# Expert weights of a mixture-of-experts layer loaded as 16 KB rows per partition, contraction reordered to match

## The chip, the cores and the metric

One core of one Trainium2 chip runs the whole kernel. The metric is the device time of one execution in microseconds (us); the kernel before has 1452.36 us as the median of three runs (1451.78 to 1454.26). Engines are named as the profile names them: PE is TensorE's products, PEld its loads of the stationary operand, DVE VectorE, ACT ScalarE, POOL GpSimd, SP the engine whose queue issues the loads from HBM.

## What is computed

One sequence of 256 tokens with 1,024 features, all in float32, passes an attention layer with two branches, a mixture of 32 experts, a gated embedding, and then a second block of two layers. The change touches the experts:

```python
def routed_experts(h, w_router, b_router, w_gate_up, b_gate_up, w_down, b_down):
    logits = hf @ w_router + b_router
    top_vals, top_idx = lax.top_k(logits, 4)          # 4 of 32 experts per token
    top_w = jax.nn.softmax(top_vals, axis=-1)
    ...                                               # rows of 64 tokens per expert
    gu = xb @ w_gate_up[e] + b_gate_up[e]             # [64,1024] @ [1024,2048]
    g, u = gu[:, :1024], gu[:, 1024:]
    g, u = jnp.minimum(g, 7.0), jnp.clip(u, -7.0, 7.0)
    glu = g * jax.nn.sigmoid(1.702 * g)
    yr = ((u + 1.0) * glu) @ w_down[e] + b_down[e]    # [64,1024] @ [1024,1024]
    ...                                               # weighted sum back to the tokens
```

## The kernel before

The 256 tokens are two tiles (`NT`) of 128 rows; X is their residual stream, XS the normed rows (token on the partition, feature along the row). The stage of the experts goes over all 32 in turn, each with one block of 64 rows (`SL`); experts with more rows get further blocks in a loop behind the stage, whose count is known only on the chip.

For an expert e, `expert` first asks for its weights with `load`. `load` (L167) cuts a matrix of 128-row blocks into tiles and issues a DMA for each on SP's queue: for gate and up one block of 128 rows x 2,048 columns makes a tile of 1 MB, 8 KB in each partition; for down two blocks of 128 x 1,024 make one, two runs of 4 KB in each partition. So an expert has 8 + 4 tiles. In the stage they come from a ring of 17 tiles (`raw_slot`, pool `ring2`), opened where the pool `p1` of the first phase is closed: a ring tile lies over that pool's buffers and waits until these are left. A pool of the next phase, `p3`, then lies over the ring. The first weights of the gated embedding (`w_ple_gate`, loaded at L193 in `load_split`) are scaled by ScalarE into its buffers (L198).

`gather` (L773) makes, for each token tile, a 0/1 matrix OH of token by row, and multiplies XS by it: for each of the 8 groups k of 128 features, `XS[:, t, k*P:(k+1)*P]` is the stationary operand [128 x 128] and OH the moving one [128 x 64]. The 16 products of an expert (32 records of PE in the trace, two for each) leave the features of group k on the partitions. DVE multiplies them by the gain `g_ffn` (L782) into XG. The gather of expert e+1 is issued behind the gate/up products of expert e; on PE it stands between the transposes of u and the products with down.

The gate/up products take XG[:, k] (64 columns) as stationary operand and halves of 512 columns of the weights as moving one, 8 x 4 = 32 products, in bank pG for gate and pU for up, behind a product with the biases (BIAS). The lower 64 partitions of a bank hold columns 0 to 511, the upper ones 512 to 1,023. VectorE and ScalarE make u from them; PE transposes the routing weights OW (L810) and four pieces of u (L823, `u[:, c*P:(c+1)*P]`), and 16 products with down follow. `combine` (L835) multiplies the result by the transposed weights and VectorE adds it to X (L840).

All operands are float32. In the trace the names right of the arrow are the moving and the stationary operand: `bank<-raw,mid` is a product with weights, `bulk<-OH,XS` the gather, `bank<-cst,mid` the transposes of u, `bulk<-mid,small` combine. The order on the engines is a scheduler's: it takes instructions of the program in order, but those under `issue_after` behind a marked one. Behind experts 18 and 22 come two extra pieces (`down_biases`, `further_list`); in the last but one expert the products of `w_ple_proj`.

Of the kernel before, what the change touches and what calls it, by code (L numbers as in the profile page):

```python
# [22 lines left out]
SL = 64  # L23
# [6 lines left out]
# columns of the constants that depend on shapes alone  # L30
# [4 lines left out]
# columns of the small vectors (feature k * 128 + p at partition p, column k)  # L35
COLS = (("g_mix", 8), ("c_2", 8), ("mla_q_lat_norm", 2), ("mla_kv_lat_norm", 1), ("g_ffn", 8), ("g_ple", 8),
        ("g_pre_2", 16), ("b_ada_2", 48), ("pool_scale_2", 8), ("w_conv_2", 24), ("mla_q_norm", 1), ("mla_k_norm", 1))
# [5 lines left out]
# rows that every partition gets  # L43
# [31 lines left out]
def layouts(inp):  # L75
    """The small inputs and the activations, laid out by partition."""
    def by_part(n):
        v = inp[n].reshape(-1)
        if v.size == QK:  # the rotated part of the heads has its gains in the rope tables
            v = np.concatenate([v[:NOPE], np.ones(P - NOPE, np.float32)])  # L80
        return v.reshape(-1, P).T

    rows = np.concatenate([inp[n].reshape(-1) for n, _ in ROWS])
    post = np.stack([inp["g_post_2"], inp["b_ada_2"][:, 2 * D:]], 1)
    return {
        "cst": constants(),
        "xT": np.ascontiguousarray(inp["x"][0].T.reshape(KD, P, S).transpose(1, 0, 2)),
        "pT": np.ascontiguousarray(inp["p"][0, 0].T.reshape(2, P, S).transpose(1, 0, 2)),
        "cols": np.ascontiguousarray(np.concatenate([by_part(n) for n, _ in COLS], 1)),
        "rows": np.ascontiguousarray(np.broadcast_to(rows, (P, R_N))),  # L90
        "post": np.ascontiguousarray(post),
    }
# [3 lines left out]
def block_kernel(ctx: ExitStack, tc: tile.TileContext, a, out, dbg=None, ne=NE):  # L96
# [19 lines left out]
    def pair(at=None):  # L116
        """Room for the halves of 1024 columns."""
        if at is not None:
            return at if isinstance(at, list) else (at[:, 0:1024], at[:, 1024:2048])
        if early.get("pair"):  # L120
            return early["pair"].pop(0)
        return [phase["pool"].tile([P, 1024], FR, name=n, tag=n, bufs=phase["pairs"]) for n in ("hi", "lo")]

    def raw_slot(n=1024):
        if "ring2" in phase:
            return phase["ring2"].tile([P, 2048], F32, name="raw2", tag="raw2")
        if early.get("raw"):
            return early["raw"].pop(0)
        return phase["pool"].tile([P, 1024], F32, name="raw", tag="raw", bufs=phase["raws"])
# [22 lines left out]
    def mm3(o, l, r, start, stop):  # L152
        """float32 product of operands split in halves of 12 bits each."""
        mm(o, l[0], r[0], start, False)
        mm(o, l[0], r[1], False, False)
        mm(o, l[1], r[0], False, stop)

    def split(raw, dst, eng=None):
        """raw = dst[0] + dst[1], both exact in the tensor engine's short float32."""
        nc.scalar.copy(dst[0], raw)  # L160
        n = raw.shape[-1]
        w = n if eng is None or len(raw.shape) > 2 else min(n, 512)
        for c0 in range(0, n, w):
            cs = slice(c0, min(n, c0 + w))
            (eng or nc.vector).tensor_sub(dst[1][..., cs], raw[..., cs], dst[0][..., cs].bitcast(F32))  # L165

    def load(src, cn, size=2048, at=None):  # L167
        """Rows of src over (k, partition), a tile at a time, in turn in the tiles at where they are given."""
# [14 lines left out]

    def load_split(src, cn, order=None, room=(), eng=None, gains=None, later=None, raws=None):
        """As load, each tile in two halves; with gains, rows by themselves, times those,
        and what makes the low halves in the list later."""
# [24 lines left out]
    tiles = {"adr": [ada_slot() for _ in range(3)]}  # L211
    hh, hl = [slot(s, dt=FR).rearrange("p (k n) -> p k n", k=KD) for s in ("s0", "s1")]
# [4 lines left out]
    wu, vv = slot("s2", 2560), slot("s5")  # L217
# [146 lines left out]
    # the rotated part of the keys that the heads share  # L364
# [6 lines left out]
    def rope(dst, src, T, half_, eng=None):  # L371
        """dst = src * cos + swapped src * sin, for heads [128, heads, 2 * half_] with the table of a token tile."""
# [7 lines left out]
    def head_root(src, hd, extra=None):  # L380
        """(mean of squares + eps) ** -0.5 of the heads [128, heads, d] over hd features."""
        ss, d = tiny([P, H], "ssh"), src.shape[2]
        for h0 in (0, 4):
            sq = mid([P, 4, d])
            nc.scalar.activation(sq, src[:, h0:h0 + 4], AF.Square)
            nc.vector.reduce_sum(ss[:, h0:h0 + 4], sq, axis=AX)
        if extra is not None:
            nc.vector.tensor_scalar(ss, ss, extra, None, op0=OP.add)
        return root(mean_eps(ss, hd, H)).unsqueeze(2)

    roots_a, marks = [], []  # what fills gaps is issued behind the marks
# [32 lines left out]
    # the norm along the tokens, on every partition  # L424
# [61 lines left out]
    def values(hp, prs, Vt, dst):  # L486
        """The values of two heads, feature-major, in halves."""
# [42 lines left out]
    MODC = perm.tile([P, 2, 16], F32, name="MODC")  # L530

    def ada_acc(l, c, e):
        """The products of 512 columns, still to be summed over the partitions."""
# [58 lines left out]
    def branch_weights(n):  # L592
        """A tile for each 256 columns."""
# [5 lines left out]
    # sigmoid(z) = (tanh(z / 2) + 1) / 2; the half follows the output projection  # L599
# [23 lines left out]
    # the biases of gate and up: row p has expert p % 32's, low halves where p // 32 is odd,  # L623
    # the columns h * 512 to h * 512 + 511 of both for h = p // 64
# [31 lines left out]
    def logits(XT, h, pl):  # L656
        """The transposed half of X[:, t] times the router's weights; the norm's factor follows."""
# [72 lines left out]
    def further_list():  # L730
        """The further blocks of 64 rows of the experts that got more than 64."""
# [16 lines left out]
        # a row of the list for each partition that has one: its place, then its expert and first rank  # L748
# [24 lines left out]
    def gather(rank, wgt):  # L773
        OH, OW = [work.tile([P, NT, n], F32, name=s, tag=s, bufs=2) for s, n in (("OH", SL), ("OW", P))]
        pX = bulk()
        for t in range(NT):
            nc.vector.tensor_scalar(OH[:, t], io64, rank(t), None, op0=OP.is_equal)  # L777
            for k in range(KD):
                mm(pX[:, k * SL:(k + 1) * SL], XS[:, t, k * P:(k + 1) * P], OH[:, t], t == 0 and k == 0,
                   t == NT - 1 and k == KD - 1)  # L780
        XG = mid([P, KD, SL])
        nc.vector.tensor_mul(XG, pX.rearrange("p (k n) -> p k n", k=KD), bcol("g_ffn", 0, KD, SL))  # L782
# [6 lines left out]
    def expert(rank, wgt, biassel, gu_src, dn_src, after_gu=None, ready=None, at=None):  # L789
        gu = load(gu_src, 2 * DE, at=at)  # L790
        dn = load(dn_src, D) if at is None else None
# [4 lines left out]
        for k in range(KD):  # L796
            for i, pb in enumerate((pG, pU)):
                for h in range(2):
                    mm(pb[h * SL:(h + 1) * SL], XG[:, k], gu(k, i * DE + h * 512, i * DE + (h + 1) * 512),
# [13 lines left out]
        # what does not wait for the activations of this expert fills their time  # L813
# [6 lines left out]
        dn = dn or load(dn_src, D, at=at)  # L820
        ph = bank()
        for c in range(4):
            nc.tensor.transpose(ph[:, c * P:(c + 1) * P], u[:, c * P:(c + 1) * P], ident)  # L823
# [3 lines left out]
        for j in range(8):  # L827
            for h in range(2):
                mm(py[h * SL:(h + 1) * SL], hT[:, j % 4, (j // 4) * SL:(j // 4 + 1) * SL],
                   dn(j, h * 512, (h + 1) * 512), j == 0, j == 7)  # L830
# [52 lines left out]
    ring2 = tc.tile_pool(name="ring2", bufs=17, reuse_waits="tile")  # L883
    phase.update(ring2=ring2.__enter__())
    for e in range(ne):
        if e == max(ne - 2, 0):
            # of the gated embedding, what does not depend on the experts
            wpp, pT_ = load(a["w_ple_proj"][0], D), raw_slot()[:, :512].rearrange("p (k n) -> p k n", k=2)
# [50 lines left out]
    def split_T(t, dst, src, scale_of=None, bias_of=None):  # L939
        """src(k) of 128 columns each transposed, with per-feature scale and shift, in halves."""  # L940
# [23 lines left out]
    def products(ks, f, turned, late, free=None, behind=None):  # L964
        """The products f(k, h) in an order that frees the weights of the first four k soon,
        the last of them behind the transposes of the tokens before."""
# [32 lines left out]
    def sum_sq(t, ss):  # L999
        """Squares of X[:, t], summed by halves as they come."""  # L1000
# [5 lines left out]
    def normed(l, t, ss, hm):  # L1006
        """The modulated norm of X[:, t], transposed, in halves."""
# [14 lines left out]
    def gates_of(l):  # L1022
        """The weights of the gates that are token-major: the first tokens need not wait for the others."""
# [31 lines left out]
    for l in range(2):  # L1055
# [16 lines left out]
        def gate(dst, g, j):  # L1072
            """dst times feature tile j of the token-major g."""
# [70 lines left out]
        # the gate of the residual, on every partition, times the gains of the last norm  # L1144
# [75 lines left out]
```

## Time and profile before

| | |
|---|---|
| runs, median (lowest to highest) | 1452.36 us (1451.78 to 1454.26) |
| the profiled execution: its own time, the span of its page | 1451.8 us |
| PE busy | 1385.2 us (95%) |
| PEld / DVE / ACT / POOL busy | 795.1 / 594.2 / 319.3 / 320.9 us |
| packets on the main DMA queue | 143,936, with 500.60 MB |
| expert stage, from the first to the last product with expert weights | about 234 to 1185 us |

The page cuts the span into 40 slices of 36.3 us and gives the busy share of each engine in tenths, 9 being 90% or more. Further views list what an engine waited for, its work grouped by form of instruction, its timeline, and the DMA traffic of a stretch. One product of float32 shows as more than one record on PE; a duration "of one" is that of one record and overlaps the next, so the pace is read from starts or from a sum over many.

### The profile page before, as it was taken

Reading aid. Unit: us, or ns where it says so; the run is one execution under the profiler, and the core shown is the slowest. Engines: PE = TensorE matmul, PEld = TensorE weight load, DVE = VectorE, ACT = ScalarE, POOL = GpSimd, SP = SyncE. Lnnn points to the kernel's source line nnn. Section 1 sums busy time; section 2 is a strip of 40 time slices with the busy share of each in tenths; the row PEclk is TensorE's granted clock in tenths of the full one; section 3 lists DMA queues with packets and bytes.
Section 4 is the critical chain, followed back from the end, with each engine's and each line's share of the span. In section 5 each row is a group of like instructions: output and inputs, shape, how many; then the busy total and the mean of one; then the engine's idle time right before and its main releaser. Section 6 shows DMA issues by size and latency. Waiting matters only on the chain. (4 is left out here: it accounts for less than half of the span.)

```text
span 1451.8 us, 18980 instructions
## 1 busy us (share of the span) xinstructions
PE 1385.2 (95%) x7599; PEld 795.1 (55%) x7599; DVE 594.2 (41%) x973; ACT 319.3 (22%) x598; POOL 320.9 (22%) x353
## 2 busy tenths in 40 slices
PE   7989999999999999999999999999999998889987
PEld 6788886344444444444443344444444347887986
DVE  4898954121322132213222222221321138688685
ACT  6745531000000000000000000000001135435432
POOL 5595461000000000000000000000000035785682
PEclk9989998999999999999999999999999999999999
DMA  9738789999999999999999999999999955756651
GB/s 332 239 119 305 263 305 401 417 417 418 417 415 416 418 418 416 415 417 418 418 416 416 417 417 418 417 415 417 417 418 415 417 226 189 232 176 202 202 190 44
DMA packets 144586, 502.56 MB, mean 346 GB/s; under 512 B 10288, under 2 KB 63792, under 8 KB 111472
## 3 DMA queue, kind: packets, MB, share of 16 engines
q1 hardware_dynamic: 143936, 500.60, 88.0%
q8 instruction: 61, 1.00, 0.3%
q10 hardware_dynamic: 560, 0.72, 0.2%
q14 instruction: 29, 0.24, 0.0%
HBM read 500.24 MB, written 1.05 MB: 345 GB/s over the span
## 5 line engine op out<-in xcount | busy, mean ns | idle before, releaser
L150 PE MATMUL bank<-raw,mid 128*64 128x512 f32 x3072 | 680.3, 598 | 1.9 <-ACT mid L825 1.4
L150 PEld LDWEIGHTS bank<-raw,mid 128*64 128x64 f32 x3072 | 215.1, 138 | 414.9 <-issue 387.9
L803 DVE TENSOR_SCALAR mid<-bank 128x512 f32<-128x512 f32 x32 | 22.1, 691 | 443.7 <-PE bank L150 443.7
L855 POOL CAST BIAS<-BIAS 128x128 fp32r<-128x128 f32 x32 | 10.2, 321 | 852.5 <-PE bank L150 852.4
L165 DVE TENSOR_TENSOR lo<-raw,hi 128x1024 fp32r<-128x1024 f32 (+2 forms) x91 | 116.1, 1296 | 21.3 <-ACT hi L160 20.9
L150 PE MATMUL bulk<-OH,XS 128*128 128x64 f32 x1024 | 121.6, 278 | 1.6 <-DVE OH L777 1.6
L150 PEld LDWEIGHTS bulk<-OH,XS 128*128 128x128 f32 x1024 | 120.2, 196 | 2.6 <-DVE OH L777 1.8
L160 ACT CAST hi<-raw 128x1024 fp32r<-128x1024 f32 (+1 forms) x102 | 105.8, 1041 | 68.0 <-PE bulk L150 57.5
L805 ACT ACTIVATE mid<-mid 128x512 f32<-128x512 f32 x32 | 20.1, 629 | 390.6 <-DVE mid L803 390.6
L150 PE MATMUL bulk<-mid,small 64*128 64x512 f32 x256 | 99.2, 628 | 7.1 <-DVE X L840 6.4
L784 DVE TENSOR_SCALAR OW<-cst,RM,SW 128x128 f32<-128x128 f32 x64 | 19.3, 344 | 172.1 <-PE bank L810 172.1
L840 DVE TENSOR_TENSOR X<-X,bulk 128x512 f32<-128x512 f32 x128 | 81.7, 679 | 9.0 <-PE bulk L150 9.0
L165 POOL TENSOR_TENSOR lo<-raw,hi 128x512 fp32r<-128x512 f32 x50 | 72.9, 1484 | 40.1 <-ACT hi L160 35.3
L812 ACT COPY small<-bank 128x256 f32<-128x256 f32 x32 | 11.9, 372 | 290.2 <-PE bank L810 290.2
L150 PEld LDWEIGHTS bulk<-mid,small 64*128 64x128 f32 x256 | 31.0, 185 | 74.8 <-issue 40.4
L150 PE MATMUL bulk<-hi,s 128*128 128x256 f32 (+2 forms) x256 | 59.3, 323 | 7.9 <-ACT hi L160 7.4
L150 PE MATMUL bulk<-s,hi 128*128 128x256 f32 x320 | 63.7, 296 | 0.0
L782 DVE TENSOR_TENSOR mid<-bulk,VC 128x512 f32<-128x512 f32 x32 | 22.1, 691 | 90.9 <-PE bulk L150 90.9
L556 DVE SCALAR_TENSOR_TENSOR acc<-adr,cact,acc 128x512 f32<-128x512 f32 x49 | 55.5, 1133 | 0.8 <-DMA adr<-in_w_ada_dram 0.3
L150 PEld LDWEIGHTS bulk<-s,hi 128*128 128x128 f32 x320 | 51.8, 197 | 1.0 <-DVE s L609 0.4
L559 POOL TENSOR_TENSOR adr<-adr,cact 128x512 f32<-128x512 f32 x32 | 44.5, 1412 | 34.3 <-DMA adr<-in_w_ada_dram 34.3
L150 PEld LDWEIGHTS bulk<-hi,s 128*128 128x128 f32 x256 | 43.9, 195 | 11.6 <-ACT hi L160 7.4
(442 smaller groups left out, 1906.0 us busy)
## 6 DMA issues: line engine op xcount, KB each, us to landing
raw<-in_w_gate_up_dram SPq DMA_DIRECT2D x256, 1024.0 KB, 19.8
raw<-in_w_down_dram SPq DMA_DIRECT2D x128, 1024.0 KB, 20.0
raw<-in_w_in_dram SPq DMA_DIRECT2D x75, 512.0 KB, 5.1
adr<-in_w_ada_dram SPq DMA_DIRECT2D x48, 512.0 KB, 4.5
raw<-in_w_out_dram SPq DMA_DIRECT2D x23, 512.0 KB, 3.8
raw<-in_w_ple_gate_dram SPq DMA_DIRECT2D x5, 512.0 KB, 15.8
raw<-in_w_branch_b_dram SPq DMA_DIRECT2D x4, 512.0 KB, 7.3
raw<-in_w_branch_a_dram SPq DMA_DIRECT2D x4, 512.0 KB, 5.4
```

What stands on the lines that cost most here:

```text
L150: nc.tensor.matmul(o, l, r, start=start, stop=stop)
L160: nc.scalar.copy(dst[0], raw)
L165: (eng or nc.vector).tensor_sub(dst[1][..., cs], raw[..., cs], dst[0][..., cs].bitcast(F32))
L556: e.scalar_tensor_tensor(v, w[:, k], cact[:, i + k:i + k + 1], v, op0=OP.mult, op1=OP.add)
L559: e.tensor_mul(w[:, k:k + 2], w[:, k:k + 2], cact[:, i + k:i + k + 2].unsqueeze(2).to_broadcast([P, 2, n]))
L782: nc.vector.tensor_mul(XG, pX.rearrange("p (k n) -> p k n", k=KD), bcol("g_ffn", 0, KD, SL))
L784: nc.vector.tensor_scalar(OW[:, t], io64d, rank(t), wgt(t), op0=OP.is_equal, op1=OP.mult)
L803: nc.vector.tensor_scalar(g_, pG, 7.0, None, op0=OP.min)
L805: nc.scalar.activation(sg, g_, AF.Sigmoid, scale=1.702)
L812: nc.scalar.copy(OT, pT[:, :S])
L840: nc.vector.tensor_add(xv, xv, pc)
L855: nc.gpsimd.tensor_copy(bs, ONE[:, e, :, None].bitcast(F32).to_broadcast([P, 2, SL]))
```

## The change

The rows of an expert's matrices are dealt to the partitions in another way. `load_rows` gives partition p of block b the r rows that follow each other in HBM, from row (128 b + p) r on: two rows of 2,048 for gate and up, four rows of 1,024 for down, 16 KB in one run in both cases. A tile is 2 MB, an expert has 4 + 2 tiles, and the ring has 8 tiles of 16 KB per partition in place of 17 of 8 KB. The inner dimension of a product is summed over partitions and over j in the tile, so the other operand must follow the same order: `gather` takes every second column of XS (`k // 2 * 256 + k % 2`, step 2), the gain that scales XG is laid out likewise (`g_rows`, 8 new columns in VC), and the transposes before down take every fourth column of u. The further blocks load pieces of 8 KB per partition as before, in the new order. `vv` and `wu` are allocated earlier in `p1`, so their place changes; `w_ple_proj` and pT share one ring tile. Comments are gone, so line numbers move by 2 to 23.

```diff
+        if n == "g_rows":
+            return inp["g_ffn"].reshape(4, P, 2).transpose(1, 0, 2).reshape(P, KD)
...
-            return phase["ring2"].tile([P, 2048], F32, name="raw2", tag="raw2")
+            return phase["ring2"].tile([P, 4096], F32, name="raw2", tag="raw2")
...
+    def load_rows(src, cn, r, at=None):
+        blocks = src.rearrange("(b p r) n -> b p r n", p=P, r=r)
+        nb, parts = src.shape[0] // (P * r), {}
+        pr = r if at is None else 2048 // cn
+        def piece(b, i):
+            if (b, i) not in parts:
+                raw = (raw_slot() if at is None else at[len(parts) % len(at)])[:, :pr * cn]
+                raw = raw.rearrange("p (r n) -> p r n", r=pr)
+                nc.sync.dma_start(raw, blocks[b, :, i * pr:(i + 1) * pr])
+                parts[b, i] = raw
+            return parts[b, i]
+        if at is None:
+            for b in range(nb):
+                piece(b, 0)
+        return lambda b, j, c0, c1: piece(b, j // pr)[:, j % pr, c0:c1]
...
+    vv, wu = slot("s5"), slot("s2", 2560)
...
-    wu, vv = slot("s2", 2560), slot("s5")
...
-                mm(pX[:, k * SL:(k + 1) * SL], XS[:, t, k * P:(k + 1) * P], OH[:, t], t == 0 and k == 0,
+                mm(pX[:, k * SL:(k + 1) * SL], XS[:, t, k // 2 * 256 + k % 2:(k // 2 + 1) * 256:2], OH[:, t], t == 0 and k == 0,
...
-        nc.vector.tensor_mul(XG, pX.rearrange("p (k n) -> p k n", k=KD), bcol("g_ffn", 0, KD, SL))
+        nc.vector.tensor_mul(XG, pX.rearrange("p (k n) -> p k n", k=KD), bcol("g_rows", 0, KD, SL))
...
-        gu = load(gu_src, 2 * DE, at=at)
-        dn = load(dn_src, D) if at is None else None
+        gu = load_rows(gu_src, 2 * DE, 2, at)
+        dn = load_rows(dn_src, D, 4) if at is None else None
...
-                    mm(pb[h * SL:(h + 1) * SL], XG[:, k], gu(k, i * DE + h * 512, i * DE + (h + 1) * 512),
+                    mm(pb[h * SL:(h + 1) * SL], XG[:, k], gu(k // 2, k % 2, i * DE + h * 512, i * DE + (h + 1) * 512),
...
-            nc.tensor.transpose(ph[:, c * P:(c + 1) * P], u[:, c * P:(c + 1) * P], ident)
+            nc.tensor.transpose(ph[:, c * P:(c + 1) * P], u[:, c::4], ident)
...
-                   dn(j, h * 512, (h + 1) * 512), j == 0, j == 7)
+                   dn(j // 4, j % 4, h * 512, (h + 1) * 512), j == 0, j == 7)
...
-    ring2 = tc.tile_pool(name="ring2", bufs=17, reuse_waits="tile")
+    ring2 = tc.tile_pool(name="ring2", bufs=8, reuse_waits="tile")
...
-            wpp, pT_ = load(a["w_ple_proj"][0], D), raw_slot()[:, :512].rearrange("p (k n) -> p k n", k=2)
+            pr = raw_slot()
+            wpp, pT_ = load(a["w_ple_proj"][0], D, at=[pr[:, :2048]]), pr[:, 2048:2560].rearrange("p (k n) -> p k n", k=2)
```

On SP's queue one expert's loads in the middle of the stage, before:

```order
L176 DMA raw_5013<-in_w_gate_up_dram 128x2048
L176 DMA raw_5015<-in_w_gate_up_dram 128x2048
L176 DMA raw_5017<-in_w_gate_up_dram 128x2048
L176 DMA raw_5019<-in_w_gate_up_dram 128x2048
L176 DMA raw_5021<-in_w_gate_up_dram 128x2048
L176 DMA raw_5023<-in_w_gate_up_dram 128x2048
L176 DMA raw_5025<-in_w_gate_up_dram 128x2048
L176 DMA raw_5027<-in_w_gate_up_dram 128x2048
L176 DMA raw_5029<-in_w_down_dram 128x2x1024
L176 DMA raw_5031<-in_w_down_dram 128x2x1024
L176 DMA raw_5033<-in_w_down_dram 128x2x1024
L176 DMA raw_5035<-in_w_down_dram 128x2x1024
```

The same expert in the changed kernel:

```order
L197 DMA raw_5203<-in_w_gate_up_dram 128x4096
L197 DMA raw_5205<-in_w_gate_up_dram 128x4096
L197 DMA raw_5207<-in_w_gate_up_dram 128x4096
L197 DMA raw_5209<-in_w_gate_up_dram 128x4096
L197 DMA raw_5211<-in_w_down_dram 128x4096
L197 DMA raw_5213<-in_w_down_dram 128x4096
```

Twelve issues become six, in the same order, and nothing stands between the experts in either.

On PE, from combine of one expert to the first gate/up product after the next biases (names with a number are ring tiles), before:

```order
L150 MATMUL bulk<-mid,small 128x512 x4
L823 MATMUL bank<-cst,mid 128x128 x4
L150 MATMUL bulk<-OH,XS 128x64 x16
L150 MATMUL bank<-raw_4892,mid 64x512 x4
L150 MATMUL bank<-raw_4894,mid 64x512 x4
L150 MATMUL bank<-raw_4896,mid 64x512 x4
L150 MATMUL bank<-BIAS 128x512 x2
L810 MATMUL bank<-cst,OW 128x128 x2
L150 MATMUL bank<-raw_4898,mid 64x512 x4
L150 MATMUL bank<-raw_5013,mid 64x512 x4
```

The same place in the changed kernel:

```order
L152 MATMUL bulk<-mid,small 128x512 x4
L845 MATMUL bank<-cst,mid 128x128 x4
L152 MATMUL bulk<-OH,XS 128x64 x16
L152 MATMUL bank<-raw_5336,mid 64x512 x8
L152 MATMUL bank<-raw_5338,mid 64x512 x8
L152 MATMUL bank<-BIAS 128x512 x2
L832 MATMUL bank<-cst,OW 128x128 x2
L152 MATMUL bank<-raw_5453,mid 64x512 x8
```

The last quarter of down (raw_4898) stood behind the biases and the transposes of OW; as the second half of the tile raw_5338 it now stands before them.

## Rows read from the trace of the kernel before

**Rows 1.** The page: first line, and busy tenths of two engines
```profile
span 1451.8 us, 18980 instructions
...
PE   7989999999999999999999999999999998889987
...
DMA  9738789999999999999999999999999955756651
```
**Rows 2.** Waits of PE, 240 to 1185 us (total us, times, longest)
```profile
PE bulk L150 <- DVE X L840: 6.4, 31, 0.2
...
PE bank L150 <- DVE small L744: 0.4, 1, 0.4
```
**Rows 3.** PE's work by form, 320 to 1080 us (busy us, ns, idle)
```profile
L150 PE MATMUL bank<-raw,mid 128*64 128x512 f32 x2472 | 546.0, 597 | 0.0
```
**Rows 4.** Waits of SP's queue from 500 to 600 us
```profile
SPq L176 <- DMA raw<-in_w_gate_up_dram: 33.5, 19, 2.1
```
**Rows 5.** Timeline of PE, expert stage (start us, length us, operation, count)
```profile
484.36 3.68 PE L150 MATMUL bulk<-OH,XS 128*128 128x64 f32 x32
...
494.15 15.67 PE L150 MATMUL bank<-raw,mid 128*64 128x512 f32 x72
...
512.99 0.66 PE L823 MATMUL bank<-cst,mid 128*128 128x128 f32 x4
513.49 3.68 PE L150 MATMUL bulk<-OH,XS 128*128 128x64 f32 x32
```
**Rows 6.** DMA packets of two stretches, 779 to 794 and 767 to 774 us
```profile
DMA packets 946, 6.25 MB, mean 417 GB/s; under 512 B 96, under 2 KB 96, under 8 KB 272
...
q1 hardware_dynamic: 945, 6.23, 100.4%
...
DMA packets 658, 2.90 MB, mean 415 GB/s; under 512 B 44, under 2 KB 44, under 8 KB 563
...
q1 hardware_dynamic: 658, 2.90, 102.8%
```
**Rows 7.** Timeline of SP's queue: DMA issues, first expert and about 728 us
```profile
186.74 19.06 SPq L176 DMA_DIRECT2D raw<-in_w_gate_up_dram  x8
...
727.81 17.42 SPq L176 DMA_DIRECT2D raw<-in_w_gate_up_dram  x8
```
**Rows 8.** Timeline of PE, first expert's begin, expert 18's combine
```profile
217.54 1.91 PE L652 MATMUL bank<-cst,X 128*128 128x128 f32 x16
...
234.32 6.04 PE L150 MATMUL bank<-raw,mid 128*64 128x512 f32 x20 [0.57 <-DVE mid L782]
...
771.91 1.98 PE L150 MATMUL bulk<-mid,small 64*128 64x512 f32 x6
```
**Rows 9.** DMA issues, 238-258 and 727-746 us (count, KB, us to landing)
```profile
raw<-in_w_down_dram SPq DMA_DIRECT2D x4, 1024.0 KB, 10.5
...
raw<-in_w_gate_up_dram SPq DMA_DIRECT2D x8, 1024.0 KB, 20.8
```
**Rows 10.** PE's loads of stationary operands by form, 320 to 1080 us
```profile
L150 PEld LDWEIGHTS bulk<-OH,XS 128*128 128x128 f32 x800 | 91.3, 192 | 0.0
```
**Rows 11.** VectorE's sums by form, whole span
```profile
L386 DVE TENSOR_REDUCE ssh<-mid 128x4 f32<-128x256 f32 x12 | 4.4, 403 | 0.0
...
L675 DVE TENSOR_REDUCE SW<-small 128x32 f32<-128x128 f32 x2 | 0.7, 374 | 0.1
```
**Rows 12.** Loads of lines 823 and 417 (ns min/median/max, first, last start)
```profile
L823 PEld LDWEIGHTS bank<-cst,mid x128: 137/140/197, 253.2 to 1176.7; 128*128 128x128 f32 x128
...
L417 PEld LDWEIGHTS bank<-cst,s x32: 123/126/129, 52.9 to 79.5; 128*96 128x96 f32 x32
```
**Rows 13.** Timeline of SP's queue, end of the expert stage
```profile
1167.64 18.10 SPq L193 DMA_DIRECT2D adr<-in_w_ple_gate_dram  x3
```
**Rows 14.** Timeline of ScalarE, end of the expert stage
```profile
1185.42 1.15 ACT L198 ACTIVATE se<-raw,VC 128x1024 fp32r<-128x1024 f32 x1
...
1195.69 2.20 ACT L198 ACTIVATE hi<-adr,VC 128x1024 fp32r<-128x1024 f32 x2
```

More of the change, by code (lines that the diff above doesn't have):

```diff
@@ L36 @@
 COLS = (("g_mix", 8), ("c_2", 8), ("mla_q_lat_norm", 2), ("mla_kv_lat_norm", 1), ("g_ffn", 8), ("g_ple", 8),
-        ("g_pre_2", 16), ("b_ada_2", 48), ("pool_scale_2", 8), ("w_conv_2", 24), ("mla_q_norm", 1), ("mla_k_norm", 1))
+        ("g_pre_2", 16), ("b_ada_2", 48), ("pool_scale_2", 8), ("w_conv_2", 24), ("mla_q_norm", 1), ("mla_k_norm", 1), ("g_rows", 8))
 VCOL, _n = {}, 0
@@ L819, in expert @@
                 nxt = after_gu()
-        dn = dn or load(dn_src, D, at=at)
+        dn = dn or load_rows(dn_src, D, 4, at)
         ph = bank()
         for c in range(4):
-            nc.tensor.transpose(ph[:, c * P:(c + 1) * P], u[:, c * P:(c + 1) * P], ident)
+            nc.tensor.transpose(ph[:, c * P:(c + 1) * P], u[:, c::4], ident)
         hT = mid([P, 4, P])
```

## The prediction, made before the changed kernel ran

> **What bounds the kernel now.** I read the page from the top. Both TensorE and the DMA engines are marked full from slice 6 to slice 31, which is the expert stage [rows 1]. Busy shares alone cannot say which of two full resources sets the pace, so the next view is the waits. Over the whole stage PE's list has five entries and no DMA among them: 6.4 us for VectorE's additions in combine is the longest, 0.4 us the shortest, in 945 us [rows 2]. Grouped by operation, the weight products have 0.0 us of idle time before them in 2,472 records [rows 3]. So every weight tile was there before PE came to it. SP, which issues the loads, spends a third of 100 us waiting for earlier transfers to land [rows 4]. TensorE is the bound; the transfers are close behind.
>
> How close? One expert on PE, from one gather to the next, is 513.49 - 484.36 = 29.13 us [rows 5]. One expert in transfers is 12 x 1.0486 = 12.58 MB, at 417 GB/s [rows 6] 30.2 us. Supply is thus a little slower than use and lives on a lead. At the start the first tile is issued at 186.74 [rows 7] and used at 234.32 [rows 8]. For expert 18 the eighth tile is issued at about 727.81 + 17.42 - 0.33 = 744.9 [rows 7], lands 20.8 us later [rows 9] at 765.7, and is used in the last 8 records, 1.7 us, before combine begins at 771.91 [rows 8], so from 770.2. A lead of more than 30 us has shrunk to 4.5 us by then, and the list of waits says that it is never used up.
>
> The page's span is 1451.8 us [rows 1]; the median of the three runs is 0.5 us above. The sum below is made against the 1451.8.
>
> **The change part by part.**
>
> *Transfers.* Per expert 12 transfers of 1 MB become 6 of 2 MB, and the rows of a partition become 16 KB instead of 8 KB (gate and up) and 4 KB (down). What a packet takes I work out from two stretches with different mixtures [rows 6], leaving the 96 and 44 packets under 512 B at nothing: 176 of 4 KB and 673 of 8 KB took 16 x 15 x 1.004 = 241.0 us, 519 and 95 took 16 x 7 x 1.028 = 115.1 us; hence 0.164 us and 0.315 us. Two packets of 4 KB cost 0.013 us more than one of 8 KB. If doubling again saves as much, 16 KB takes 0.617 us, if nothing, 0.630. An expert is 64 + 64 packets per engine now, 30.7 us by these prices, of which the measured rate makes 30.2 (a factor of 0.985). After, it is 48 packets: 29.2 to 29.8 us. That is worth 0.4 to 1.0 us per expert to the DMA engines, and **nothing to the time**, because PE waits for no transfer. The trace has no 16 KB packet; both bounds come from those rows.
>
> *Ring.* 17 tiles of 1 MB become 8 of 2 MB. A tile is asked for when the one eight before is left. On PE eight tiles are 8 x 29.13 / 6 = 38.8 us; less the 3.5 us in which a 2 MB tile is used (16 records of 0.218 us: 72 in 15.67 us [rows 5]) and less some 13 us to land (10.5 us for 1 MB early in the stage [rows 9] and 2.5 us for the second MB), the lead is about 22 us. Over the 17 experts to expert 18 it would lose 17 x 0.1 = 2 us with the quick packets, 17 x 0.7 = 12 us with the slow ones. It holds either way: 0 us. The cover is this lead; without it each tile would cost its shortfall.
>
> *Start.* The ring's slots lie over what the first phase uses, in the order in which PE leaves it: the first tile over attention's values and the modulation's buffers, the second into SG, the third over the raw tiles of w_out, the other five over its halves and the merged branches. PE has left the last of these when its transposes of X begin, at 217.54 [rows 8]. So the fourth gate/up tile is issued by then at the latest and lands by 217.5 + 13 = 230.5; PE wants it at 234.32 + 3 x 3.5 = 244.8. Cost 0, with 14 us to spare.
>
> *Order on PE.* The same products in the same order but for one thing, shown ahead: the last quarter of down stood behind the biases and now stands before them. The records are the same; nothing waits between them today, and the banks that the biases fill are read much later. 0 us. VectorE swaps two pairs in one expert, ScalarE two copies that have the whole expert as cover; POOL's order is the same. 0 us.
>
> *Strided stationary operands.* Two reads change. The gather takes every second column of XS as its stationary operand (8 bytes apart), the transposes before down take every fourth of u (16 bytes apart). No load of weights with a step is in the trace, so both need bounds.
> Gather: 32 records in 3.68 us [rows 5], 114 ns each, and the loads set that: 91.3 us for 800, with no idle time before them [rows 10]. Whatever a load gains in length is paid 32 x 32 = 1,024 times. Upper end: VectorE's sum over numbers 128 bytes apart takes 374 ns for 128, its contiguous sum 403 ns for 256 [rows 11]; per number that is 1.9 times at most (whatever part of both is fixed makes it less). 0.9 x 114 ns x 1,024 = 105 us. Lower end 0; a gain has no source, as the same columns are loaded. I take 0: a strided load spans 1,024 bytes of a partition in 114 ns, 9.0 bytes per ns, and the weight products already stream 2,048 bytes in 218 ns, 9.4 bytes per ns [rows 5].
> Transposes: 4 in 513.49 - 512.99 = 0.50 us [rows 5], 125 ns each, 128 in all. Loads of 128 columns take 140 ns and of 96 columns 126 [rows 12]: 0.44 ns a column, 56 ns of streaming; the rest is latency that overlaps. 1.9 times 56 is 106 ns, still under 125: lower end 0. Upper end: the whole record stretched, 1.9 x 140 = 266 ns a piece, 141 ns x 128 = 18 us. I take 0, by the nearest row, the transposes' own loads.
>
> *End.* The last three loads of the next phase's first weights were issued from 1167.64 on, over 18 us, as PE left its last tiles [rows 13]; now their room is free when the fourth gate/up tile of expert 31 is left, about 1172. ScalarE reaches those loads only at 1195.69 [rows 14], so nothing is gained. The two output halves that now lie over the last tile are written from 1185.42 on, right after that tile, anyway [rows 14]. 0 us.
>
> **Sum:** 1451.8 + 0, and 0.5 for the median is 1452.3; I write the median itself, **1452.4 us, no change**. About 0.2% (2.9 us) is what a measurement of this kernel can tell from no change.
>
> **The rivals.**
>
> *The step in the transposes is paid* (slower). A load 16 bytes apart spans 2,048 bytes; at the 9.4 bytes per ns of the products that is 218 ns, 93 ns over today's pace, on PE's path since the engine works in order: 128 x 93 = 11.9 us, **1464**. It decides as soon as a load takes over 125 ns in flow. For it: VectorE's strided sum. Against: the short streaming part.
> [...]
>
> *The step in the gather is paid too* (slower): up to 105 + 18 us, at half of it **1514**; against it stands the rate of bytes above.
>
> *The transfers become the bound* (slower). If an expert's six transfers take more than 29.13 + 22 / 17 = 30.4 us, the lead is gone by expert 18 and PE waits for tiles twice as coarse. At 31.5 us it costs 32 x 2.4 - 22 = 54 us, **1506**; just over the point, 1455 to 1460. For it: a 16 KB packet is untried. Against: three sizes would have to break a straight line.
>
> *The packets are cut to 8 KB or less by the hardware* (it doesn't do what it says): supply 29.8 us, time **1452** all the same.
>
> *Faster:* if the earlier loads at the end let ScalarE take its three scalings of them into gaps before, 3 x 1.1 us [rows 14] come off the end, **1449**. Its queue speaks against it: other work of its own runs on up to there.
>
> **How the numbers follow.** No change 0.55, the cut packets within it; transposes 0.22; gather 0.08; transfers 0.10; faster 0.05. The forecast is the likeliest, 1452.4. The range goes from 1448.5 to 1470: the gain, no change, the transposes to their upper end of 18 us, and a transfer bound just past its point; what is left out is the gather (0.08) and the hard transfer bound (0.08). Faster 0.05, same 0.55, slower 0.22 + 0.08 + 0.10 = 0.40. The likeliest case alone reaches from 1450 to 1455.
>
> **What the next profile shows.** Right: one expert on PE still 29.1 us, no DMA in PE's waits, four transposes in 0.50 us, 32 gather records in 3.7 us, the DMA engines still near full with SP waiting for PE. Wrong: transposes in 0.9 us (first rival), gather in more than 4 us (second), a DMA name among PE's waits (third). Packets should fall by 32 x 128 x 16 - 32 x 48 x 16 = 41,000 if a row of 16 KB is one packet.

## The result, and the profile after

The changed kernel takes 1462.83 us (median of 4 runs, 1460.83 to 1463.58) beside 1452.66 us for the kernel before in the same comparison (1451.78 to 1454.26): a ratio of 1.0070 with a 95% interval from 1.0058 to 1.0082, 8.4 to 11.9 us slower. The forecast was 1452.4 us and no change; the range reached to 1470. The profiled execution is the quickest of the four; its own time is 1460.83 us beside a span of 1459.0. In e1 to e12 below the span is likewise 1.8 to 2.2 us shorter than the execution's own time. By that difference the 1451.8 of [rows 1], which the table ahead and my sum took for the time itself, belongs to an execution of some 1453.8 us (an estimate: its own time is not on record apart). The comparison of spans below is not touched by it.

The page after, the lines that answer to [rows 1], and its main queue:

```profile
span 1459.0 us, 18581 instructions
...
PE   7989999999999999999999999999999998989987
...
DMA  9738769999999999999999999999999936656651
...
q1 hardware_dynamic: 99904, 500.59, 85.6%
```

TensorE and the DMA engines are as full as before. PE's list of waits from 240 to 1190 us has again no DMA in it, and 6.4 us for VectorE's additions at its head, as in [rows 2]. The packets fell from 143,936 to 99,904: 40,960 by the longer rows, as forecast, and 3,072 small ones that went with the 192 transfers saved.

SP's queue (waits from 500 to 600 us: total us, times, longest), first the second row of the kernel before, which [rows 4] do not show, then the changed kernel,

```profile
SPq L176 <- DMA raw<-in_w_down_dram: 25.9, 13, 2.2
...
SPq L197 <- PE bank L152: 91.0, 21, 10.8
```

and the packets:

```profile
DMA packets 2934, 42.78 MB, mean 428 GB/s; under 512 B 323, under 2 KB 323, under 8 KB 323
...
q1 hardware_dynamic: 2931, 42.73, 100.5%
```

SP waits for PE alone now, 91 us in 100. Before, it spent 33.5 + 25.9 = 59.4 us of the 100 on earlier transfers, more than the third that I had read from the first of the two rows; that is gone. 2,931 - 323 packets carried 42.7 MB in 16 x 100 x 1.005 = 1,608 us: 0.617 us for one of 16 KB, the quick bound of the estimate. The transfers got better as forecast, and were as hidden as forecast.

The timeline of PE (start us, length us, operation, count), beside [rows 5]:

```profile
485.65 0.74 PE L845 MATMUL bank<-cst,mid 128*128 128x128 f32 x4
486.23 3.88 PE L152 MATMUL bulk<-OH,XS 128*128 128x64 f32 x32
490.04 7.09 PE L152 MATMUL bank<-raw,mid 128*64 128x512 f32 x32
...
515.06 0.75 PE L845 MATMUL bank<-cst,mid 128*128 128x128 f32 x4
515.64 3.88 PE L152 MATMUL bulk<-OH,XS 128*128 128x64 f32 x32
```

One expert takes 515.64 - 486.23 = 29.41 us instead of 29.13. The four transposes take 0.58 us instead of 0.50 (486.23 - 485.65), the gather, up to the first product with down, 490.04 - 486.23 = 3.81 instead of 3.61 (before, the row behind 513.49 begins at 517.10). 0.08 + 0.20 = 0.28 us are the whole difference; 32 times that is 9.0 us, inside the measured 8.4 to 11.9.

The loads by form, 320 to 1080 us (count, busy us, mean ns, idle before), beside [rows 10, 12]:

```profile
L152 PEld LDWEIGHTS bulk<-OH,XS 128*128 128x128 f32 x800 | 96.5, 197 | 0.0
...
L845 PEld LDWEIGHTS bank<-cst,mid 128*128 128x128 f32 x100 | 13.9, 209 | 19.0 <-issue 18.2 <-DVE mid L829 0.8
```

A gather load takes 96.5 / 800 = 120.6 ns instead of 114.1, a load for a transpose 209 ns instead of 140, of which the pace shows 145 ns (0.58 us / 4) instead of 125. Of the other forms that every expert uses, none moved by more than 4 ns a load.

The 145 and 125 ns are averages of four. The records of the transposes (ns min/median/max, first and last start), before and after:

```profile
L823 PE MATMUL bank<-cst,mid x128: 272/273/330, 253.4 to 1176.9; 128*128 128x128 f32 x128
...
L845 PE MATMUL bank<-cst,mid x128: 283/283/387, 253.4 to 1185.9; 128*128 128x128 f32 x128
```

The longest is the first of each four, 57 ns longer than before. The other three are 10 ns longer, and in the trace they follow each other after 120 ns instead of 109. So some 56 of the 88 ns that the four pay per expert are paid once, at the first, and only about 11 ns by each step from there.

From expert 0's transposes to expert 31's the profiled execution is 8.9 us longer, 1185.41 - 253.40 against 1176.47 - 253.35. Behind the stage it is 1.7 us shorter, but e2 below gives that no weight.

### The profile page after: what moved, and what is told of

Read it like the earlier page. It is cut to its first block, busy times and chain, and to the rows that moved or that the text cites. A ratio compares the mean times of both kernels' runs of the same rounds, so it can differ in the third digit from the quotient of the medians.

```text
span 1459.0 us, 18581 instructions
## 1 busy us (share of the span) xinstructions
PE 1392.6 (95%) x7599; PEld 804.9 (55%) x7599; DVE 595.2 (41%) x973; ACT 319.2 (22%) x598; POOL 320.2 (22%) x353
## 3 DMA queue, kind: packets, MB, share of 16 engines
q1 hardware_dynamic: 99904, 500.59, 85.6%
## 5 line engine op out<-in xcount | busy, mean ns | idle before, releaser
L152 PE MATMUL bulk<-OH,XS 128*128 128x64 f32 x1024 | 127.7, 284 | 1.6 <-DVE OH L799 1.6
L152 PEld LDWEIGHTS bulk<-OH,XS 128*128 128x128 f32 x1024 | 126.6, 201 | 2.6 <-DVE OH L799 1.8
L854 ACT COPY mid<-bank 128x512 f32<-128x512 f32 x32 | 18.8, 587 | 320.7 <-PE bank L152 320.7
L167 POOL TENSOR_TENSOR lo<-raw,hi 128x512 fp32r<-128x512 f32 x50 | 72.2, 1470 | 40.6 <-ACT hi L162 35.8
```

Of the source, the lines that this page charges most:

```text
L152: nc.tensor.matmul(o, l, r, start=start, stop=stop)
L854: nc.scalar.copy(yr, py)
```

## The experiments

The runs of one group are compared with runs of the kernel before on the same chip. Theory S is that the loads pay for the step itself; theory T, its rival, that TensorE reads slower because of what the transfers now write.

### The step without the transfers, the transfers without the step

`e1_before_steps`, the kernel before with both steps:

```diff
-                mm(pX[...], XS[:, t, k * P:(k + 1) * P], OH[:, t], ...
+                mm(pX[...], XS[:, t, k // 2 * 256 + k % 2:(k // 2 + 1) * 256:2], OH[:, t], ...
-            nc.tensor.transpose(ph[:, c * P:(c + 1) * P], u[:, c * P:(c + 1) * P], ident)
+            nc.tensor.transpose(ph[:, c * P:(c + 1) * P], u[:, c::4], ident)
```

> The kernel before, with its 17 tiles of 1 MB and its transfers, but the two stationary operands read with the step (every second column of XS, every fourth of u). The contraction then pairs features with other features' weights; the number and shape of all instructions are those of before. Theory S (the loads pay for the step, whatever is transferred): a gather load 121 instead of 114 ns, four transposes 0.58 instead of 0.50 us, one expert 29.41 instead of 29.13 us, 32 times 0.28 us, the time 1461.5 +- 1. Theory T (transfers with 16 KB rows disturb TensorE's reads of SBUF, the step itself is free): 29.13 us and 1452.5, as before.

`e2_after_no_steps`, the changed kernel with the reverse of that edit:

> The changed kernel, with both stationary operands read in one piece as before (again other features are paired with the weights; transfers, ring and order are the change's). Theory S: one expert 29.13 us, the time 1452.5 +- 1, and the ring and the transfers alone worth nothing. Theory T: 29.41 us and 1461 to 1463.

`e3_after_gather_step`, the changed kernel with the reverse in the transposes alone:

> The changed kernel with the step in the gather alone, u read in one piece. Theory S, with the sizes read from the two profiles (gather 6.6 ns x 1,024 = 6.7 us, transposes 20 ns x 128 = 2.6 us): 1459.5 +- 1. If the transposes were the larger part, as my first rival had it: under 1456. Theory T: 1461 to 1463.

Measured: e1 1460.25 us (1.0061, 1.0048 to 1.0074), e2 1453.01 (1.0005, 0.9996 to 1.0014), e3 1459.59 (1.0049, 1.0036 to 1.0062), before 1452.09. The timeline of PE in e1:

```profile
486.13 0.75 PE L823 MATMUL bank<-cst,mid 128*128 128x128 f32 x4
486.72 3.88 PE L150 MATMUL bulk<-OH,XS 128*128 128x64 f32 x32
...
516.13 3.88 PE L150 MATMUL bulk<-OH,XS 128*128 128x64 f32 x32
```

The same in e2:

```profile
485.85 0.66 PE L845 MATMUL bank<-cst,mid 128*128 128x128 f32 x4
486.34 3.68 PE L152 MATMUL bulk<-OH,XS 128*128 128x64 f32 x32
...
515.47 3.68 PE L152 MATMUL bulk<-OH,XS 128*128 128x64 f32 x32
```

With old transfers and the step, one expert is 516.13 - 486.72 = 29.41 us; with new transfers and no step, 515.47 - 486.34 = 29.13. Theory T is out; e1 alone lies 0.25 us under its expected interval. Of the two parts of the step, e3 against e2 gives the gather 6.6 us (6.7 expected); e7 below has the transposes' part alone. The ring, the 2 MB tiles, the moved quarter of down and the end of the stage are worth between -0.04% and 0.14% together in e2, so the 1.7 us by which the tail of the one profiled execution was shorter are no gain of the change.

### How a load pays

`e5_gather4_turn2` and `e6_gather8_turn3`, the changed kernel with longer steps in the gather and shorter ones in the transposes (the two operands side by side, cut out of their lines):

```diff
-XS[:, t, k // 2 * 256 + k % 2:(k // 2 + 1) * 256:2]      u[:, c::4]
+XS[:, t, k // 4 * 512 + k % 4:(k // 4 + 1) * 512:4]      u[:, c // 2 * 256 + c % 2:(c // 2 + 1) * 256:2]
...
+XS[:, t, k::8]                                           u[:, c * 32:c * 32 + 382:3]
```

> The changed kernel with steps of 16 bytes in the gather (every fourth column of XS) and 8 bytes in the transposes (features are paired with other weights; the count of the work is the same). [...] Theory B (by bytes spanned, at 9.4 bytes per ns): 2,048 bytes in 218 ns, 7.0 us, about 1560.

> The same with 32 bytes in the gather (every eighth column) and 12 bytes in the transposes. [...] Theory B: 4,096 bytes in 436 ns, 14 us per expert, about 1780.

Measured: 1625.46 and 1635.38 us, one run each. The timeline of PE in e5:

```profile
493.18 0.75 PE L845 MATMUL bank<-cst,mid 128*128 128x128 f32 x4
493.76 7.61 PE L152 MATMUL bulk<-OH,XS 128*128 128x64 f32 x32
501.31 9.78 PE L152 MATMUL bank<-raw,mid 128*64 128x512 f32 x32
```

The same in e6:

```profile
497.02 0.74 PE L845 MATMUL bank<-cst,mid 128*128 128x128 f32 x4
497.59 7.79 PE L152 MATMUL bulk<-OH,XS 128*128 128x64 f32 x32
505.31 8.14 PE L152 MATMUL bank<-raw,mid 128*64 128x512 f32 x32
```

The gather takes 501.31 - 493.76 = 7.55 us at 16 bytes and 505.31 - 497.59 = 7.72 at 32: 236 and 241 ns a load. Theory B had 218 and 436; that 32 bytes cost nearly what 16 cost speaks against it. A transpose's load went up by 69 ns at 16 bytes (140 to 209), a gather's by 122, so the one is no measure of the other. The transposes show 0.58 us at 8 bytes and 0.57 at 12, beside 0.50 without a step: they pay the same, some 20 ns each on average, for any of the three steps. In flow a transpose comes every 120 ns at 16 bytes, where a gather load takes over 230; why two kinds of load answer so differently stays open. 32 x 3.94 us of longer gathers are 126 of the 172 us that e5 is over e2, and the transposes' step is 2.6. Most of the rest is in the clock, by stretches of e5 (length, then busy us and count of PE, PEld, DVE, ACT, POOL, the granted clock, DMA share and GB/s):

```profile
494.00:496.10 2.10, 2.10 (x11) 2.10 (x10) 0.47 (x1) 0.55 (x1) 0.00 (x0) 1.00 1.00 429
498.00:500.10 2.10, 2.10 (x11) 2.10 (x10) 0.00 (x0) 0.00 (x0) 0.00 (x0) 0.50 1.04 445
...
505.00:508.00 3.00, 3.00 (x12) 0.85 (x12) 0.00 (x0) 0.00 (x0) 0.00 (x0) 0.71 0.00 0
508.00:511.00 3.00, 3.00 (x16) 0.76 (x12) 0.00 (x0) 0.00 (x0) 0.00 (x0) 1.00 0.84 224
```

While the gather runs at this pace, the granted clock falls from 1.00 to 0.50, and it is back at 1.00 from 508 on; the 32 records of down behind the gather take 9.78 us there, and 8.1 to 9.8 over the stage, instead of 7.09. The loads of this gather, those that lie before the clock falls and those behind it:

```profile
494.09 2.66 PEld L152 LDWEIGHTS bulk<-OH,XS 128*128 128x128 f32 x11
...
496.89 4.30 PEld L152 LDWEIGHTS bulk<-OH,XS 128*128 128x128 f32 x18
```

The last load's own 0.33 us taken off, 10 paces of 233 ns are left at a granted clock of 1.00 and 17 of 234 at 0.50. **A load with 16 bytes of step does not follow the clock.**

The two half gathers of expert 0 run at 0.50 in all three kernels: that is the granted clock of 224 to 234.2 us before and after, and of 224 to 233.5 in e5. The loads of the second half, 16 of them, first in the kernel before, then in the changed one, then in e5:

```profile
229.86 3.49 PEld L150 LDWEIGHTS bulk<-OH,XS 128*128 128x128 f32 x16 [0.93 <-DVE OH L777]
```

```profile
229.81 3.49 PEld L152 LDWEIGHTS bulk<-OH,XS 128*128 128x128 f32 x16 [0.93 <-DVE OH L799]
```

```profile
229.77 3.81 PEld L152 LDWEIGHTS bulk<-OH,XS 128*128 128x128 f32 x16 [0.93 <-DVE OH L799]
```

The last load's own 0.33 us taken off, 15 paces are left: 211 ns without a step, 211 with 8 bytes, 232 with 16. The same for a gather of 32 at a granted clock of 1.00, in the changed kernel and in the kernel before:

```profile
486.12 3.86 PEld L152 LDWEIGHTS bulk<-OH,XS 128*128 128x128 f32 x32
```

```profile
513.38 3.65 PEld L150 LDWEIGHTS bulk<-OH,XS 128*128 128x128 f32 x32
```

Less the last 0.20 and 0.19 us, 31 paces: 118 ns with 8 bytes, 112 without. So the step of 8 bytes costs 6 ns at a granted clock of 1.00 and nothing at 0.50, and a load at 16 bytes takes some 233 ns at either. A load in one piece goes with the clock (112 and 211 ns), one at 16 bytes does not; what sets its time is not shown. An estimate from these numbers: half the step at half of 233 would be 117 ns, a little over the 112 and far under the 211 of a load in one piece. It fits the 118 and the 211 at 8 bytes; it does not fit twice the step (241 ns at 32 bytes) or the transposes (120 ns in flow at 16), and no run tests it apart from the loads that it is made from.

### Writing the operands in the dealt order

`e4_after_dealt`, the changed kernel with the step moved to VectorE's writes of XS and of u:

```diff
-        nc.vector.tensor_scalar(XS[:, t], X[:, t], r, None, op0=OP.mult)
+        nc.vector.tensor_scalar(XS[:, t].rearrange("q (b j p) -> q b j p", b=4, j=2),
+                                X[:, t].rearrange("q (b p j) -> q b j p", b=4, j=2), r, None, op0=OP.mult)
...
-        nc.vector.tensor_mul(u, u, sg)
+        nc.vector.tensor_mul(g_.rearrange("p (c i) -> p c i", c=4), u.rearrange("p (i c) -> p c i", c=4),
+                             sg.rearrange("p (i c) -> p c i", c=4))
...
```

In the lines left out here the gather and the transposes read the two operands in one piece again.

> The changed kernel, with the two operands written in the dealt order once, so that TensorE reads them in one piece: the normed XS by VectorE with a step of 8 bytes (2 instructions in all), the last multiplication of u by VectorE with a step of 16 bytes (one per expert). Theory S: TensorE is back at 29.13 us per expert, 1452.5 +- 1, if VectorE's product with the step, which may take up to twice its 0.7 us, still has the cover of combine. If it has not: 32 x up to 0.7 = 22 us, up to 1475. Theory T: 1461 to 1463.

`e7_after_xs_dealt`, the first of the two edits alone, so that the transposes keep their step:

> The changed kernel with XS written in the dealt order (VectorE reads X with a step of 8 bytes, twice in all), so that the gather reads in one piece; the transposes keep their step, VectorE its plain product. Theory: gather back at 114 ns a load, transposes still 0.58 us, one expert 29.21 us; 1453 + 32 x 0.08 = 1455.6 +- 1. If what e4 paid lay in XS and not in VectorE's slower product of u, it shows again here: 1459.

Measured: e4 1459.22 us (1.0043, 1.0030 to 1.0056; its runs lie between 1454.84 and 1460.91), e7 1457.55 (1.0034, 1.0022 to 1.0047), before 1452.09 and 1453.18. VectorE's work in e4 and PE's loads there, 320 to 1080 us (count, busy us, mean ns, idle before):

```profile
L830 DVE TENSOR_TENSOR mid<-mid 128x512 f32<-128x512 f32 x25 | 26.7, 1069 | 0.0
```

```profile
L152 PEld LDWEIGHTS bulk<-OH,XS 128*128 128x128 f32 x800 | 91.2, 192 | 2.8
```

e4 has its loads back at 114 ns, but VectorE's product takes 1,069 ns instead of 685, the additions to X behind it come 0.38 us later, and the gather's loads then have 2.8 / 25 = 0.11 us of idle time before them. That they wait for the bank which these additions free is read from the order of the program; the row names no releaser. One expert takes 29.27 us, 0.14 more than before, 4.5 of the 7.1 us; at the end of the stage in the profiled execution the clock was 0.83 for 10 us (expert 31's products with down took 8.78 us instead of 7.09), which makes 1.7 more. The cover of combine that the expectation asked for was not there. XS costs VectorE nothing: its two instructions take 0.75 us in both orders. In e7 an expert takes 29.22 us, as expected (29.21) and 0.09 more than in e2, which is the transposes' step alone; and the time is 2 us above the expected. Some of that is again a place where PE waits and the clock falls: expert 18 to 19, with the biases of down, takes 38.3 us in e7's profile, 36.6 in e2's and 38.1 before, and the mean granted clock of 775 to 818 us is 0.92, 0.96 and 0.92.

### What combine waits for

`e8_before_pool_u`, the kernel before with the last product of u on POOL:

```diff
-        nc.vector.tensor_mul(u, u, sg)
+        nc.gpsimd.tensor_mul(u, u, sg)
```

> The kernel before, with the last product of u on POOL instead of VectorE. If VectorE's queue holds combine (0.21 us of waiting per expert in both kernels, and 0.1 us more in e4, where its product of u took 0.4 us longer), the additions to X come 0.7 us sooner and the wait goes: 31 x 0.21 = 6.4 us, 1446. With PE at 28.92 us per expert the transfers at 30.2 use the lead up by expert 18 (4.5 us less 17 x 0.21 = 0.9 left), so a DMA may appear among PE's waits. If POOL's product (1.4 us on the page) is not done when the transposes begin, 32 x up to 0.7 us come on: up to 1475.

Measured: 1478.78 us (1.0178, 1.0158 to 1.0198). PE's waits from 240 to 1190 us:

```profile
PE bank L150 <- ACT mid L825: 21.0, 31, 0.7
PE bulk L150 <- DVE X L840: 7.9, 30, 0.3
```

The wait for VectorE did not go, 7.9 us: the first addition to X stands behind another product of VectorE that is still there. And the scheduler, with u expected later, put the transposes behind the gather, where ScalarE's copy of their result has no cover: 21.0 us in 31 waits. My expectation named a late u and not the order.

`e9_before_spare` gives combine a fourth bank and fixes the order, on the kernel before; `e10_dealt_spare` is the same on e7:

```diff
-                    pc = bulk()
+                    pc = spare() if (t, h) == (0, 1) else bulk()
...
-            if after_gu:
-                nxt = after_gu()
...
+        if after_gu:
+            with tc.issue_after(nc.cur_bb.bb.instructions[-1]):
+                nxt = after_gu()
         hT = mid([P, 4, P])
```

> The kernel before, with the second of combine's four products in the bank that is spare in this stage, and the next gather issued behind the transposes of u, where it stood anyway. Theory C (the 0.21 us that PE waits in every combine is the fourth product's wait for the bank of the first): the wait goes, 28.92 us per expert, 1452.4 - 31 x 0.21 = 1446. The lead of the transfers shrinks to 4.5 - 17 x 0.21 = 0.9 us at expert 18, so a few tenths of DMA waits are possible there. Otherwise (the wait moves to the gather's bank or to u): 29.13 and 1452.4.

> The same edit on the changed kernel with XS written in dealt order (e7, 1457.5). Theory C: 29.22 - 0.21 = 29.01 us per expert, 1457.5 - 6.5 = 1451; no DMA among PE's waits. Otherwise 1457.5.

Measured: e9 1456.66 us (1.0035, 1.0022 to 1.0048), **e10 1448.67** (0.9977, 0.9968 to 0.9985), before 1451.48. The same edit makes the kernel before slower and takes 7 to 9 us off e7 (8.9 between the two times, 7.2 when each is set against its own runs of the kernel before). Timeline of PE in e10, first expert and middle of the stage:

```profile
252.60 1.13 PE L844 MATMUL bank<-cst,mid 128*128 128x128 f32 x4 [2.32 <-DVE mid L830]
253.53 6.92 PE L152 MATMUL bulk<-OH,XS 128*128 128x64 f32 x32
```

and

```profile
485.51 0.69 PE L152 MATMUL bulk<-mid,small 64*128 64x512 f32 x1
...
488.39 0.72 PE L844 MATMUL bank<-cst,mid 128*128 128x128 f32 x4 [0.89 <-DVE mid L830]
...
517.22 0.72 PE L844 MATMUL bank<-cst,mid 128*128 128x128 f32 x4 [0.89 <-DVE mid L830]
```

One expert takes 517.22 - 488.39 = 28.83 us, 0.39 less than in e7; e9 has 28.74, 0.39 less than before. Theory C named 0.21 and is right in part. The wait for the bank is gone from PE's list, but another has come, 240 to 1190 us in e10 (e9 has the same):

```profile
PE bank L844 <- DVE mid L830: 29.9, 32, 2.3
```

Combine and the transposes behind it in e7, beside the rows of e10 above:

```profile
512.20 1.98 PE L152 MATMUL bulk<-mid,small 64*128 64x512 f32 x6
...
515.44 0.75 PE L846 MATMUL bank<-cst,mid 128*128 128x128 f32 x4
```

From the start of combine to that of the transposes e7 takes 3.24 us and e10 2.88 (488.39 - 485.51), of which 0.89 are the new wait for VectorE's last product of u. So combine itself became shorter by more than the wait that C named, and u is what PE waits for now. No run takes the bank and the order apart.

At its first expert the edit costs some 7 us in both: PE waits 2.32 us for u, and the gather behind that wait takes 6.92 us instead of 3.68. In the kernel before, this one gather stood ahead of the transposes (249.73 and 253.35 us) and covered the wait, so "where it stood anyway" in the expectation does not hold for the first expert. What parts the two kernels is at the end. Waits of PE in e9, 240 to 1190 us:

```profile
PE bank L150 <- DMA raw<-in_w_gate_up_dram: 7.4, 14, 0.6
```

A piece of its timeline, expert 29:

```profile
1118.19 5.50 PE L150 MATMUL bank<-raw,mid 128*64 128x512 f32 x24
1124.24 1.94 PE L150 MATMUL bank<-raw,mid 128*64 128x512 f32 x8 [0.55 <-DMA raw<-in_w_gate_up_dram]
```

From expert 26 on the last gate/up tiles of each expert come late, most of them by 0.55 us, two tiles at first and six in expert 29; an expert takes 30.1 us there, which is the transfers' own pace (12.58 MB at the 417 GB/s of 500 to 600 us in e9). The lead of [rows 7 to 9] is used up, later than I expected (expert 18) and then for good. The 9.7 us that 25 experts gained are less than the 7 lost at the first expert and the 9 lost from expert 26 on. e10 has no DMA among PE's waits.

### The transfers when PE is faster

`e11_before_half_gather` and `e12_after_half_gather`: the second token tile is left out of the gather, in the kernel before and in e2.

```diff
-        for t in range(NT):
+        for t in range(1):
             nc.vector.tensor_scalar(OH[:, t], io64, rank(t), None, op0=OP.is_equal)
...
```

> The kernel before, with the gather of the second token tile left out (8 of 16 products; half of the tokens are missing from the experts' inputs), which makes PE faster by about 1.8 us per expert, to 27.3. What the transfers then allow: 402.7 MB at 417 GB/s are 966 us from about 190 on, so the last weights land at about 1156 instead of being used at 1177, and the kernel ends near 1435, with DMA waits on PE from about expert 13 on. If transfers were not the next limit: 1452 - 32 x 1.8 = 1395.

> The changed transfers and ring with operands read in one piece (e2, 1453.0) and the same half of the gather left out. 402.7 MB at 428 GB/s are 941 us, from about 202 on (three tiles by 217): the last weights land at about 1143, the end near 1421, 14 us before e11's. If the ring of 8 held the transfers back (slots late), as late as e11 or later; if PE were still the bound, 1395 for both.

Measured: e11 1443.04 us, e12 1426.84 (2 runs each; before 1451.48). PE's waits from 240 to 1190 us in e11:

```profile
PE bank L150 <- DMA raw<-in_w_gate_up_dram: 36.3, 71, 1.5
```

and in e12:

```profile
PE bank L152 <- DMA raw<-in_w_gate_up_dram: 28.1, 31, 2.5
```

Both are bound by transfers: in the middle an expert takes 30.1 us in e11 and 29.4 in e12, which are 12.58 MB at 417 and at 428 GB/s. They lie 16.2 us apart, 14 were expected; both are 6 to 8 us later than expected. e12 reaches this limit first, at expert 7 (e11 at expert 8), which fits a smaller lead of the smaller ring; no run tests the ring apart.

## Why the prediction was right in part, and where it failed

The time lies inside the range, but not by what the range was made for: it went to 1470 for transposes that pay their whole stretch and for a transfer bound, and neither came. The likeliest case alone ended at 1455, and the 1462.83 comes from two terms that the sum put at 0. That the range held it is luck as far as the mechanism goes.

- *TensorE is the bound, the transfers are close behind*: right, though SP's share of waiting for transfers was read too low (59 us in 100, not a third). No DMA stands in PE's waits after, and e11 and e12 show the limit behind.
- *Transfers, 0.4 to 1.0 us per expert for the DMA engines and nothing to the time*: right, with the quick price (0.617 us; 29.4 us per expert against 30.1 in e12 and e11). e2 shows the nothing.
- *Ring, start, order on PE, end: 0 us*: right together, by e2 (0.9996 to 1.0014).
- *Gather, "I take 0"*: this step failed, and it carries 6.4 to 6.7 of the 9.0 us. A load went from 114 to 121 ns (from 112 to 118 by its pace), 1,024 times. The bounds (0 to 105 us) held it. The reason given for the lower end, 9.0 bytes per ns against 9.4 of the products, did not: by e5 and e6, twice the span costs 241 ns instead of 236, so bytes spanned are not what a load pays for.
- *Transposes, "I take 0"*: this failed too, with 20 ns each on average, 2.6 us. The estimate of 56 ns of streaming per load, stretched to 106, would have stayed covered; the load got 69 ns longer, and of that 56 ns showed once per expert, at the first of the four, and some 11 at each step behind it.
- *First rival, the transposes' step paid, 1464*: its time is near the result, its mechanism is not. It put 11.9 us on the transposes, which pay 2.6, and nothing on the gather. The gather rival, at 1514, had the place right and the size some 8 times too high (half of 105 us against 6.6). A forecast of "no change" beside rivals of +12 and +62 left out a small payment at the place that is paid 1,024 times.

## What to carry to other kernels

A cost of a few ns is settled by how often it is paid and by what stands beside it: a load that sets the pace (no idle time before it, busy as long as its products) pays for a step at once (here 6.6 us for 8 bytes, 1,024 times, e3 against e2), so an operand that is read a thousand times should be written in its reading order once, as e7 does with XS. A gain in a resource that is not the bound has no time of its own (0.617 us a packet of 16 KB instead of an estimated 0.630 for two of 8 KB, and e2 within 0.14% of before) but it is room for the next edit: the fourth bank of combine lost 5 us on the old transfers and took 7 to 9 us off on the new ones (e9, e10). An edit that makes an operand later or earlier may also move the scheduler's order, and the order can cost more than the edit (21.0 us of waits in e8).

## What was not expected of the hardware

A load of 128 columns of float32 with a step of 16 bytes takes some 233 ns at a granted clock of 1.00 and of 0.50, one in one piece 112 and 211. Four transposes take 0.58, 0.57 and 0.58 us with steps of 8, 12 and 16 bytes, beside 0.50 without; at 16 some 56 ns of it come at the first of four and 11 at each step behind it. VectorE reads with 8 bytes of step for nothing (0.75 us for 1,024 columns) and with 16 bytes on both inputs at 1,069 instead of 685 ns. And behind the wait of 2.32 us in PE's stream (e10) the granted clock is 8 tenths on the page, as the mean of 253.2 to 289.4 us, where the changed kernel has 9, and the gather there took 6.92 us instead of 3.68 and the 32 records of down behind it 8.30 instead of 7.09; in e5 it fell from 1.00 to 0.50 while the slow gather ran, and down took 9.78. So a wait or a slow load can cost more than its length: 3.24 + 1.21 us beside the 2.32, 2.69 beside the 3.94.
